# A hybrid backbone layer on one core: gate buffers, the block decays' row scale, the merges' buffers and the place of the 32-block solve

## The chip, the cores and the metric

The kernel runs on one core of a Trainium2 chip. The core has five engines with instruction streams of their own: TensorE (matmuls; PE in the profile, PEld for its weight loads), VectorE (DVE), ScalarE (ACT), GpSimd (POOL) and SyncE (SP, which here only issues DMAs). They meet through semaphores; each executes its own instructions strictly in the order in which they stand in the program. DMAs are issued from the queues of SP and of ScalarE. The metric is the device time of one execution in microseconds; a median over runs is given. Lower is better.

## The reference

One layer (DEPTH is 1) over 256 latent tokens and 256 context tokens of width 1024, all in float32: a half-step SwiGLU, a mixer, another half-step SwiGLU. The mixer runs two branches on the same projected input, a bidirectional gated delta rule (8 heads of 128) and a bidirectional Mamba-2 state-space scan (32 heads of 64, 2 groups), and merges them by sigmoid gates. The latent scan starts from the context's final state. The part that the change touches is the delta rule's triangular solve:

```python
    g = jnp.cumsum(blocks(g), axis=-1)
    decay = jnp.exp(jnp.where(causal, g[..., :, None] - g[..., None, :], -jnp.inf))
    kb = k * beta[..., None]
    a_mat = jnp.where(strict, jnp.einsum('bnhid,bnhjd->bnhij', kb, k) * decay, 0.0) + jnp.eye(CHUNK, dtype=f32)
    rhs = jnp.concatenate([v * beta[..., None], kb * jnp.exp(g)[..., None]], axis=-1)
    sol = lax.linalg.triangular_solve(a_mat, rhs, left_side=True, lower=True, unit_diagonal=True)
```

and, around it, in one call for each direction of each branch:

```python
    f = mixer_features(h, w_in[i], ...)
    o, _ = gdn_mixer(f, gdn_A_log[i], gdn_dt_bias[i], s_gdn)
    y, _ = ssd_mixer(f, mb_A_log[i], mb_dt_bias[i], s_mb)
    merged = jax.nn.sigmoid(ga) * (ya @ w_branch_gdn) + jax.nn.sigmoid(gb) * (yb @ w_branch_mb)
```

Queries, keys and values pass a depthwise convolution of five taps and SiLU first; queries and keys are normalised. The chunk is 64 tokens.

## The kernel before

The program goes through the adaptive-norm vectors and the first SwiGLU (until about 445 us), the mixer (until about 1050 us) and the second SwiGLU. A matmul in float32 precision is made of three passes with the operands split in a high and a low part (hH, hL, whi, wlo; lines L213 to L215): ScalarE copies a 512 KB weight tile to whi (L198), VectorE subtracts to get wlo (L202), both out of a ring of four raw tiles that SP loads (L192). Gates and zA are projected in one pass from the raw tile (`projf`, L611): 8 matmuls of 128x256 for each of 16 gate tiles.

*Keys and solve.* `keys` goes over the eight heads: a projection of 512 columns (256 context and 256 latent tokens), the convolution (`conv_silu`: L630 on VectorE is one tap, L635 the closing SiLU product, whose output is kcv for keys and cv for values), normalisation (L861, L872, L875) and the Gram matrices pg of each 128 tokens (L896). The Gram block goes by ScalarE's copy (L898) and a store (L899) to DRAM (Gsd), and comes back (L905) as N: 256 diagonal 32x32 blocks, 2 for each of 128 partitions. `block_decay` makes the matching decays D (two tiles of 32x32 entries for each partition): difference of the cumulated decays (L917, VectorE), a triangular select (L918, GpSimd), an exponential (ScalarE) and a product with -beta of the row, nb (L921, GpSimd). `elim` multiplies N by D (L963) and runs 30 steps of forward substitution, each one product into etmp (L967) and one addition to N (L970), all on VectorE. It stores the inverse blocks to DRAM (L973, Tsd).

*Merges.* `merge(s)`, for each of four pairs of 128-token tiles, one for each direction, reads those blocks back (L1102: TD and TT) and puts the 32-blocks together to 128x128 triangles. Lm holds Gram blocks, RA and RB decays (loaded from gsd, two subtractions on VectorE each, L1114, an exponential on ScalarE, L1116), which GpSimd multiplies into Lm (L1117). TensorE then goes through pTx (L1126), pTw (L1133), pTx (L1139), pTa, pTz and pTu. The zeros of TT and TD are written by VectorE (L1084 to L1088). `chain_step(s)` runs the scan over the pairs; steps 2 and 3 are the latent tokens and use `decay` (L932: a select by GpSimd into E, eight exponentials, a product with q k^T at L1200).

*Other work of that stretch.* `g_gen` is one gate tile: projection (L611), tanh on ScalarE (gth, L1071), store to gsc from ScalarE's queue (L1072). `dts` makes the step sizes of the state-space branch (softplus as a chain of 128x256 operations, L737 to L749, then pcd). `abdt` makes beta and the cumulated decays. v, q, xs, B, C, zB and zA are projected after the keys; then the state-space branch (`ssd_diag`, VectorE-heavy) and the two branches' output.

*What sets the order.* The functions emit their instructions in the order of the string PLAN (a token like `18/g5` sets the priority 18 and emits five gates; `k3` three keys; `13/m0` merge 0), and a scheduler then puts the instructions of each engine in an order by these priorities and by its own model of when each one is ready. So a change of PLAN, of a buffer or of an engine moves many instructions. A tile comes from a pool by a tag with a number of buffers, and a new tile of a tag waits until the last reader of the tile that held the buffer is done. The tags of this change: tZ, 2 buffers (gth, zth, dtx, dte); c4, 2 buffers (D, then the decays' gr and E); t4, 2 buffers (RA among others); tL, 2 buffers (sel, RB, dtz, dtg). PSUM tiles have tags too: mg has 2 banks (prow, pcd, the merges' products).

## Time and profile before

| | |
|---|---|
| time, median of 3 runs | 1342.9 us |
| the runs | 1342.9, 1339.09 and 5015.55 us |
| the profiled execution | 1346.67 us |
| its span (first to last instruction) | 1345.0 us |
| mean granted TensorE clock | 0.97 |
| busy: TensorE / VectorE / ScalarE / GpSimd | 96% / 71% / 37% / 12% |
| last key's Gram block (L896) | 516.75 us |
| solve: first product (L963) to last step (L970) | 528.35 to 591.01 us |
| first merge's first matmul (L1126) | 601.50 us |
| third run of the three | an outlier, which the median leaves aside |

The profile is of one execution on the chip. Rows of a timeline give start and duration in us, the engine, the line, the operation, the tile written and the tiles read, the shape, how many instructions stand in the row, and in brackets the engine's idle time ahead of it and what ended it. A float32 matmul is counted twice in the trace (a gate's 8 matmuls as 16). Durations of matmuls overlap, since they are pipelined: their pace is the difference of two starts. A row of the chain of waits gives start, duration, engine, tile and line. `SPq` is SP's queue.

### The profile page before, as it was taken

Reading aid. Unit: us, or ns where it says so; the run is one execution under the profiler, and the core shown is the slowest. Engines: PE = TensorE matmul, PEld = TensorE weight load, DVE = VectorE, ACT = ScalarE, POOL = GpSimd, SP = SyncE. Lnnn points to the kernel's source line nnn. Section 1 sums busy time; section 2 is a strip of 40 time slices with the busy share of each in tenths; the row PEclk is TensorE's granted clock in tenths of the full one; section 3 lists DMA queues with packets and bytes.
Section 4 is the critical chain, followed back from the end, with each engine's and each line's share of the span. In section 5 each row is a group of like instructions: output and inputs, shape, how many; then the busy total and the mean of one; then the engine's idle time right before and its main releaser. Section 6 shows DMA issues by size and latency. Waiting matters only on the chain.

```text
span 1345.0 us, 21303 instructions
## 1 busy us (share of the span) xinstructions
PE 1290.2 (96%) x8224; PEld 1108.4 (82%) x8224; DVE 955.1 (71%) x1666; ACT 501.3 (37%) x935; POOL 155.1 (12%) x123
## 2 busy tenths in 40 slices
...
GB/s 363 92 179 221 118 188 242 233 109 235 214 106 102 110 178 242 193 184 192 153 128 80 93 174 164 150 183 125 162 144 226 174 191 190 192 189 185 179 185 79
DMA packets 133018, 230.27 MB, mean 171 GB/s; under 512 B 46706, under 2 KB 78898, under 8 KB 132788
## 3 DMA queue, kind: packets, MB, share of 16 engines
...
## 4 chain that ended last, share of the span: by engine, by line
PE 64%; issue 15%; DVE 13%; DMA 5%; ACT 1%; POOL 1%; SPq 1%; DVEq 0%; POOLq 0%; ACTq 0%
PE acc L213 16%; PE acc L214 16%; PE acc L215 16%; PE acc L611 3%; PE pada L301 2%; DVE Es L1437 2%; DVE cv L630 2%; DVE Es L1426 1%; PE pn L1227 1%; PE pP L1218 1%; PE pS L1253 1%; DMA Es<-asd 1%; PE pTx L1139 1%; PE ptm L980 1%; DVE Es L1439 1%
## 5 line engine op out<-in xcount | busy, mean ns | idle before, releaser
L198 ACT CAST whi<-raw 128x1024 fp32r<-128x1024 f32 (+1 forms) x208 | 214.4, 1033 | 448.9 <-PE acc L214 397.7
L213 PE MATMUL acc<-hH,whi 128*128 128x512 f32 (+1 forms) x976 | 346.5, 357 | 3.6 <-ACT hH L432 1.8
L214 PE MATMUL acc<-hL,whi 128*128 128x512 f32 (+1 forms) x976 | 345.7, 354 | 0.0
L215 PE MATMUL acc<-hH,wlo 128*128 128x512 f32 (+1 forms) x976 | 344.8, 354 | 0.0
L202 DVE TENSOR_TENSOR wlo<-raw,whi 128x1024 fp32r<-128x1024 f32 (+1 forms) x208 | 251.3, 1210 | 96.1 <-ACT whi L198 94.3
L213 PEld LDWEIGHTS acc<-hH,whi 128*128 128x128 f32 x976 | 186.5, 191 | 27.8 <-ACT hH L432 2.2
L215 PEld LDWEIGHTS acc<-hH,wlo 128*128 128x128 f32 x976 | 186.6, 191 | 23.9
L214 PEld LDWEIGHTS acc<-hL,whi 128*128 128x128 f32 x976 | 186.6, 191 | 22.9
L270 DVE CUSTOM_DVE_ANT_0 junk<-wadat,cs 128x1024 f32<-128x1024 f32 x80 | 97.8, 1222 | 42.4 <-DMA wadat<-in_wadaT 41.7
L214 PE MATMUL acc<-aL,whi 128*128 128x256 f32 (+1 forms) x384 | 122.9, 323 | 0.0
L215 PE MATMUL acc<-aH,wlo 128*128 128x256 f32 (+1 forms) x384 | 122.3, 323 | 0.0
L213 PE MATMUL acc<-aH,whi 128*128 128x256 f32 (+1 forms) x384 | 122.2, 323 | 0.0
L630 DVE SCALAR_TENSOR_TENSOR cv<-cbuf,cc,cv 128x512 f32<-128x512 f32 (+1 forms) x144 | 107.3, 752 | 4.6 <-ACT cv L628 2.6
L611 PE MATMUL acc<-hF,raw 128*128 128x256 f32 x416 | 97.7, 391 | 8.4 <-ACT gth L1071 7.8
L611 PEld LDWEIGHTS acc<-hF,raw 128*128 128x128 f32 x416 | 80.8, 197 | 22.7 <-ACT gth L1071 9.1
L214 PEld LDWEIGHTS acc<-aL,whi 128*128 128x128 f32 x384 | 73.0, 190 | 5.6
L215 PEld LDWEIGHTS acc<-aH,wlo 128*128 128x128 f32 x384 | 72.7, 190 | 5.7
L213 PEld LDWEIGHTS acc<-aH,whi 128*128 128x128 f32 x384 | 72.6, 190 | 5.6
L567 DVE SCALAR_TENSOR_TENSOR xl<-acc,hg,xl 128x256 f32<-128x256 f32 x64 | 30.3, 482 | 47.0 <-PE acc L215 46.5
L1049 PE MATMUL acc<-raw,hF 128*128 128x512 f32 x128 | 59.4, 606 | 0.6 <-DVE zbt L1053 0.6
L372 POOL TENSOR_TENSOR sqa<-sqa,sqb 128x256 f32<-128x256 f32 x12 | 11.5, 962 | 410.6 <-ACT sqb L370 407.7
L1049 PEld LDWEIGHTS acc<-raw,hF 128*128 128x128 f32 x128 | 24.6, 194 | 30.5 <-issue 28.4
...
## 6 DMA issues: line engine op xcount, KB each, us to landing
...
```

What stands on the lines that cost most here:

```text
L198: nc.scalar.copy(hi, raw)
L202: engs[i % len(engs)].tensor_tensor(lo[:, c:c + w], raw[:, c:c + w], hi[:, c:c + w].bitcast(F32), op=ALU.subtract)
L213: mm(acc, wh, xh, start=start, stop=False)
L214: mm(acc, wh, xl, start=False, stop=False)
L215: mm(acc, wl, xh, start=False, stop=stop)
L270: self.nc.vector.tensor_tensor_reduce(out=self.junk, in0=w, in1=self.cs[s], scale=1.0, scalar=0.0, op0=ALU.mult, op1=ALU.add, accum_out=out)
L301: nc.tensor.matmul(pa[:, c], w[c][:, q * P:q * P + P], self.cTs[:, q], start=q == 0, stop=q == KD - 1)
L567: nc.vector.scalar_tensor_tensor(out=xs, in0=acc[:, NL * s - g0:NL * s - g0 + NL], scalar=hg[s][:, m:m + 1], in1=xs, op0=ALU.mult, op1=ALU ...
L611: self.nc.tensor.matmul(acc, w[:, k * P:k * P + P], self.hF[:, k], start=k == 0, stop=k == KD - 1)
L630: nc.vector.scalar_tensor_tensor(out=u3, in0=buf[:, 0:R, j:j + 64], scalar=cw[:, j:j + 1], in1=u3, op0=ALU.mult, op1=ALU.add)
L1049: nc.tensor.matmul(accs[t], self.hF[:, k, sl], w[:, wsl], start=k == 0, stop=k == 7)
L1437: V.scalar_tensor_tensor(out=B[:, j], in0=cb(1), scalar=col(self.dt, 1, j), in1=B[:, j], op0=ALU.mult, op1=ALU.add)
```

## The change

The rotation of some buffers and the place of some work change; what is computed stays the same, with the same matmuls.

- PLAN: the solve (`elim`) is emitted behind g5, dts, v2 and three further gates. The sixteen gates stay; the ten that followed v2 are split in three ahead of the solve and seven behind it.
- `g_gen`: gth gets a tag of its own with two buffers.
- `block_decay` loses the row product by nb. A new function `row_scale`, emitted just ahead of `elim`, transposes sel1 into a PSUM tile of its own, reduces it to nb and multiplies both D tiles on VectorE. sel1 becomes a constant tile, and the transpose and reduction of nb leave `abdt`.
- `keys`: the store of the Gram block is issued from ScalarE's queue and not from SP's.
- `merge`: six memsets for each merge go from VectorE to GpSimd, and RA takes a c4 buffer (where D was) and not a t4 buffer.

```diff
--- before.py
+++ after.py
@@ -28,7 +28,7 @@
 TAGS = dict(tA=4, tS=3, tL=2, tM=2, tZ=2)
 T4 = 2
 NCV = 2
-PLAN = """10/k3 block_decay k6 5/elim 18/g5 13/dts 20/v2 g10 v7 13/m0 14/m1 13/chain_start s0 s1 m2 m3 22/q9
+PLAN = """10/k3 block_decay k6 18/g5 13/dts 20/v2 g3 row_scale 5/elim 20/g7 v7 13/m0 14/m1 13/chain_start s0 s1 m2 m3 22/q9
     B_part 27/x17 25/lat_h 22/C_part 30/zB5 g17 zA9 chain_out 13/s2 s3 14/gdn_norm 15/ssd_pre h40 51/y0 gdn_out y1 70/mb_out"""
 NG = 5
 GQ = 0
@@ -80,7 +80,6 @@
 L2B = ("tr",)
 KL = ("dve",)
 MDE = 'vg'
-BDE = "vg"
 
 ADA_PE = [(k, c) for k in range(8) for c in range(2) if c or k < 4]
 
@@ -771,7 +770,8 @@
         V.tensor_scalar(out=alog, in0=alog, scalar1=-1.0, scalar2=None, op0=ALU.mult)
 
         gb = self.t2([P, 64], "gb", tag="tM")
-        sel = [self.t2([P, 16, 4, 2], f"sel{i}", tag="tL") for i in range(2)]
+        sel = [self.t2([P, 16, 4, 2], "sel0", tag="tL"), C([P, 16, 4, 2], "sel1")]
+        self.sel1 = sel[1]
         for q in sel:
             nc.gpsimd.memset(q, 0.0)
         halves = slice(0, 64), slice(64, P)
@@ -797,18 +797,15 @@
         V.tensor_copy(gc, pc[:, 0])
         for hb, hs in enumerate(halves):
             V.tensor_copy(sel[0][hs, :, :, hb], pc[hs, 0].rearrange("p t u -> p u t"))
-        pr = self.smp([P, 3, P], "prow", "mg")
+        pr = self.smp([P, 2, P], "prow", "mg")
         nc.tensor.transpose(pr[0:64, 0], gb, self.ident)
-        for i, q in enumerate(sel):
-            q = q.rearrange("p u t b -> p (u t b)")
-            nc.tensor.transpose(pr[:, 1 + i], q, self.ident)
+        nc.tensor.transpose(pr[:, 1], sel[0].rearrange("p u t b -> p (u t b)"), self.ident)
         rows = self.t2([64, P], "rows", tag="tM")
         nc.scalar.copy(rows, pr[0:64, 0])
         nc.scalar.dma_start(self.gsd, rows)
 
         self.gn, self.nb = C([P, 64], "gn"), C([P, 64], "nb")
-        for i, q in ((1, self.gn), (2, self.nb)):
-            V.tensor_reduce(out=q, in_=pr[:, i].rearrange("p (b c) -> p c b", b=2), op=ALU.add, axis=AX.X)
+        V.tensor_reduce(out=self.gn, in_=pr[:, 1].rearrange("p (b c) -> p c b", b=2), op=ALU.add, axis=AX.X)
         V.tensor_scalar(out=self.gn[64:P], in0=self.gn[64:P], scalar1=-1.0, scalar2=None, op0=ALU.mult)
         self.gcA = C([P, 4, 16], "gcA")
         V.tensor_copy(self.gcA, gc)
@@ -896,7 +893,7 @@
                 nc.tensor.matmul(pg[:, t], kT[:, ts], kT[:, ts], start=True, stop=True)
             G = kb([P, 4, P])
             nc.scalar.copy(G, pg)
-            nc.sync.dma_start(self.Gsd[h, :, 0:P].rearrange("t r c -> r t c"), G)
+            nc.scalar.dma_start(self.Gsd[h, :, 0:P].rearrange("t r c -> r t c"), G)
             if h in NB:
                 h0 = max([0] + [q + 1 for q in NB if q < h])
                 src = self.Gsd[h0:h + 1].rearrange("h t r c -> (h t r c)").rearrange("(p s x) -> p s x", s=2, x=32 * (P + 1))
@@ -908,8 +905,8 @@
     def block_decay(self):
 
         nc, G = self.nc, self.nc.gpsimd
-        gn, nb = self.gn, self.nb
-        BS, BM = (nc.vector if c == "v" else G for c in BDE)
+        gn = self.gn
+        BS = nc.vector
         self.D = []
         for sb in range(2):
             D = self.c4([P, 32, 32], "D")
@@ -918,8 +915,17 @@
             G.affine_select(out=D, in_=D, pattern=[[1, 32], [-1, 32]], base=0, channel_multiplier=0,
                             compare_op=ALU.is_gt, fill=-1e30)
             nc.scalar.activation(D, D, AF.Exp)
-            BM.tensor_tensor(D, D, self.bc(nb[:, 32 * sb:32 * sb + 32], 32, 32), op=ALU.mult)
             self.D.append(D)
+
+    def row_scale(self):
+
+        nc, V = self.nc, self.nc.vector
+        pr = self.smp([P, P], "prow", "mg")
+        nc.tensor.transpose(pr, self.sel1.rearrange("p u t b -> p (u t b)"), self.ident)
+        nb = self.nb
+        V.tensor_reduce(out=nb, in_=pr.rearrange("p (b c) -> p c b", b=2), op=ALU.add, axis=AX.X)
+        for sb, D in enumerate(self.D):
+            V.tensor_tensor(D, D, self.bc(nb[:, 32 * sb:32 * sb + 32], 32, 32), op=ALU.mult)
 
     def decay(self, t, d):
 
@@ -1067,7 +1073,7 @@
     def g_gen(self):
         for m in range(16):
             acc = self.projf("wg", m)
-            th = self.t2([P, NL], "gth", tag="tZ")
+            th = self.tp.tile([P, NL], F32, tag="gth", bufs=2, name="gth")
             self.nc.scalar.activation(th, acc, AF.Tanh, scale=0.5)
             self.nc.scalar.dma_start(self.gsc[m], th)
             yield
@@ -1081,14 +1087,15 @@
         idl, idh = self.ident[lo, lo], self.ident[hi, hi]
         TT = [self.tt([P, 8, P], f"TT{d}") for d in range(2)]
         TD = self.t2([P, 8, 64], "TD", tag="tM")
-        V.memset(TT[0][hi, :, lo], 0.0)
-        V.memset(TT[1][lo, :, hi], 0.0)
+        Z0 = nc.gpsimd.memset
+        Z0(TT[0][hi, :, lo], 0.0)
+        Z0(TT[1][lo, :, hi], 0.0)
         for r in (0, 64):
-            V.memset(TT[1][r:r + 32, :, r + 32:r + 64], 0.0)
-            V.memset(TD[r:r + 32, :, 32:64], 0.0)
+            Z0(TT[1][r:r + 32, :, r + 32:r + 64], 0.0)
+            Z0(TD[r:r + 32, :, 32:64], 0.0)
         Lm = self.tp.tile([P, 16, 96], F32, tag="lm", bufs=1, name="Lm")
         L21, L10 = Lm[:, :, 0:64], Lm[:, :, 64:96]
-        RA, RB = self.t4([P, 16, 64], "RA"), self.t2([P, 16, 32], "RB", tag="tL")
+        RA, RB = self.c4([P, 16, 64], "RA"), self.t2([P, 16, 32], "RB", tag="tL")
         q4 = [slice(32 * i, 32 * i + 32) for i in range(4)]
         c2 = [slice(0, 32), slice(32, 64)]
         part = lambda d, q: TD[q4[q], :, c2[q % 2]] if d == 0 else TT[1][q4[q], :, q4[q]]
```

Where these move instructions, on TensorE behind the last key's Gram block (L611 is a gate matmul, L980 a transpose of a value tile, L843, L844 and L850 belong to `dts`). Before, from 12 projection matmuls behind that block to the last gate of this stretch:

```order
L611 MATMUL acc<-hF,raw 128x256 x8
L980 MATMUL ptm<-ident,cv_3398 128x128 x4
L611 MATMUL acc<-hF,raw 128x256 x20
L843 MATMUL pcd<-dtg,UT 128x4x32
L843 MATMUL pcd<-dtg,LT 128x4x32
L844 MATMUL pcd<-dtg,ones 128x256
L611 MATMUL acc<-hF,raw 128x256 x11
L850 MATMUL prow<-ident,gc 128x128
L611 MATMUL acc<-hF,raw 128x256 x41
```

Now, from the last key's Gram block on (L893 is L896 of before, L610 is L611, L986 is L980):

```order
L893 MATMUL pg<-kT 128x128 x4
L610 MATMUL acc<-hF,raw 128x256 x5
L986 MATMUL ptm<-ident,cv_3396 128x128 x4
L610 MATMUL acc<-hF,raw 128x256 x17
L986 MATMUL ptm<-ident,cv_3397 128x128 x4
L610 MATMUL acc<-hF,raw 128x256 x58
```

The same 80 gate matmuls stand there, now without `dts`' products, which have moved ahead, among the keys. Ahead of the Gram block TensorE has 12 more projection matmuls of the values than before.

On TensorE at the first merge's first matmul (pTx; 128x512 is a projection of values, 128x256 one of queries). Before:

```order
L213 MATMUL acc<-hH_3151,whi 128x512
L214 MATMUL acc<-hL_3153,whi 128x512
L215 MATMUL acc<-hH_3151,wlo 128x512
L1126 MATMUL pTx<-ident,TD 32x32 x8
L1126 MATMUL pTx<-ident,TT_4671 32x32 x8
L1126 MATMUL pTx<-ident,TD 32x32 x8
L1126 MATMUL pTx<-ident,TT_4671 32x32 x8
```

and now (L1133 is L1126 of before):

```order
L212 MATMUL acc<-hH_3151,whi 128x256
L213 MATMUL acc<-hL_3153,whi 128x256
L214 MATMUL acc<-hH_3151,wlo 128x256
L1133 MATMUL pTx<-ident,TD 32x32 x8
L986 MATMUL ptm<-ident,cv_3397 128x128 x4
L212 MATMUL acc<-hH_3067,whi 128x256
L213 MATMUL acc<-hL_3069,whi 128x256
```

Before, no query projection stands ahead of the first merge; now 72 matmuls of it do, and 16 more transposes of values.

On VectorE at the beginning of the solve (L963 is the product with D, L967 and L970 a step; L746 to L749 and L840 belong to `dts`; L630 and L635 to a value's convolution). Before:

```order
L963 TENSOR_TENSOR N<-N,D 128x1024 x2
L630 SCALAR_TENSOR_TENSOR cv_3399<-cbuf_3293,cc,cv_3399 128x512
L746 SCALAR_TENSOR_TENSOR dt<-dt,dtz 128x256
L967 TENSOR_TENSOR etmp<-N 128x60
L630 SCALAR_TENSOR_TENSOR cv_3399<-cbuf_3293,cc,cv_3399 128x512
L747 SCALAR_TENSOR_TENSOR dt<-dt,dte 128x256
L970 TENSOR_TENSOR N<-N,etmp 128x2x30
L749 SCALAR_TENSOR_TENSOR dt<-dt,dtx 128x256
L967 TENSOR_TENSOR etmp<-N 128x116
L635 SCALAR_TENSOR_TENSOR cv_3399<-cv_3399 128x512
L840 TENSOR_TENSOR dtg<-dt,alogs 128x256
L970 TENSOR_TENSOR N<-N,etmp 128x2x29x2
```

and now (L969, L973 and L976 are L963, L967 and L970 of before; L1121 is L1114):

```order
L969 TENSOR_TENSOR N<-N,D 128x1024 x2
L973 TENSOR_TENSOR etmp<-N 128x60
L976 TENSOR_TENSOR N<-N,etmp 128x2x30
L973 TENSOR_TENSOR etmp<-N 128x116
L976 TENSOR_TENSOR N<-N,etmp 128x2x29x2
L973 TENSOR_TENSOR etmp<-N 128x168
L976 TENSOR_TENSOR N<-N,etmp 128x2x28x3
L973 TENSOR_TENSOR etmp<-N 128x216
L976 TENSOR_TENSOR N<-N,etmp 128x2x27x4
L973 TENSOR_TENSOR etmp<-N 128x260
L976 TENSOR_TENSOR N<-N,etmp 128x2x26x5
L973 TENSOR_TENSOR etmp<-N 128x300
```

The solve's first steps stand next to each other now. The operations of `dts` stand among the keys, the first subtraction of RA behind the eleventh half-step, and the subtractions of the first RB pairs ahead of the solve. Behind this piece, among the later steps, stand 20 convolution taps (12 before) and nine weight splits (six before).

## The prediction

> **What bounds the kernel now.** I read the page first, then TensorE's and VectorE's busy time in stretches, then TensorE's timeline where it stands idle, then the chain and the queues of that place. The page:
>
> ```profile
> PE 1290.2 (96%) x8224; PEld 1108.4 (82%) x8224; DVE 955.1 (71%) x1666; ACT 501.3 (37%) x935; POOL 155.1 (12%) x123
> ```
>
> TensorE is busy for 1290.2 of 1345.0 us. The change takes no matmul away, so all that it can win are TensorE's 55 us of idle time and the time at a lower clock. Stretches (PE, PEld, DVE, ACT, POOL busy, then the granted clock, the DMA share and GB/s) show where that is in the part that the change reorders, from about 445 to 1050 us:
>
> ```profile
> 475.00:500.00 25.00, 20.96 (x106) 18.58 (x105) 20.97 (x27) 14.20 (x40) 10.44 (x6) 0.87 0.90 186
> 525.00:550.00 25.00, 17.15 (x70) 14.36 (x69) 19.49 (x35) 6.78 (x16) 3.44 (x2) 0.80 0.71 160
> 950.00:975.00 25.00, 19.65 (x58) 9.96 (x57) 23.30 (x51) 6.69 (x14) 10.36 (x9) 0.86 0.35 120
> ```
>
> Two of the holes are ones that the change aims at. TensorE's timeline:
>
> ```profile
> 494.20 1.12 PE L861 MATMUL l2t<-ident,kcv 128*128 128x128 f32 x4 [4.04 <-DVE kcv L635]
> 497.67 6.59 PE L611 MATMUL acc<-hF,raw 128*128 128x256 f32 x24
> 516.75 1.05 PE L896 MATMUL pg<-kT 128*128 128x128 f32 x8
> 535.73 8.11 PE L611 MATMUL acc<-hF,raw 128*128 128x256 f32 x24 [7.85 <-ACT gth L1071]
> 549.41 18.25 PE L611 MATMUL acc<-hF,raw 128*128 128x256 f32 x82
> 601.50 0.69 PE L1126 MATMUL pTx<-ident,TD 32*32 32x32 f32 x16
> ```
>
> L611 is a gate: 8 matmuls, which the trace counts as 16. At full clock one record takes 18.25 / 82 = 0.223 us, a matmul 0.445, a gate 3.56. Behind both waits the clock is down: the 24 records at 535.73 take 8.11 us and not 5.35 (2.8 lost), those at 497.67 6.59 (1.2 lost, and some 1.8 more in the three rows ahead, since the L896 pass there takes 1.92 us against 1.05 at 516.75, and L861 and L875 twice their usual time). So the second hole costs 7.85 + 2.8 = 10.6 us, the first 4.04 + 3.0 = 7.0.
>
> But work of another kind is nearly as late as TensorE there. The chain of waits from the last key's Gram block (L896) to the 32-block solve on VectorE, and the solve's end with the queue that carries it to the first merge:
>
> ```profile
> 516.91 0.91 PE pg L896 x8
> 517.84 0.60 ACT kb L898
> 518.45 4.03 DMA Gsd<-kb
> 523.86 4.49 DMA Lm<-Gsd
> 528.35 2.36 DVE N L963 x2
> ...
> 590.79 0.22 DVE L970 TENSOR_TENSOR N<-N,etmp 128x60 f32<-128x60 f32 x1
> ...
> 591.03 0.33 SPq L973 DMA_DIRECT2D Tsd<-N  x1
> 596.61 1.80 SPq L1102 DMA_DIRECT2D TD<-Tsd  x4
> 598.46 2.45 SPq L1102 DMA_DIRECT2D TT<-Tsd  x5
> ```
>
> The solve runs from 528.35 to 591.0. Its blocks are stored and loaded back by SP; the TT loads are issued until 600.9, and the merge's first matmul (L1126) starts at 601.50. TensorE came there without idle time, so it was not early: the solve was ready with it, to within a microsecond. Whoever takes 10.6 us from TensorE ahead of that place must also bring the solve forward, or TensorE waits at L1126 instead.
>
> **The change part by part.** *Own buffers for the gates' tanh.* Before, gth takes turns with dtx and dte in tZ, so a gate's tanh waits until VectorE is done with the dt chain, which itself is spread around the solve's start:
>
> ```profile
> 510.88 0.29 DVE L836 COPY dtx<-dt 128x256 f32<-128x256 f32 x1 [4.79 <-DMA gsc<-gth]
> 531.29 2.56 DVE L746 SCALAR_TENSOR_TENSOR dt<-dt,dtz 128x256 f32<-128x256 f32 x1
> 535.11 1.28 DVE L749 SCALAR_TENSOR_TENSOR dt<-dt,dtx 128x256 f32<-128x256 f32 x1
> DMA to landing us min/median/max: 2.2/3.5/6.7
> ```
>
> The wait at 535.73 ends with dtx's last reader, L749. With two own buffers a tanh waits only for the store of the gate two before it; that store lands in 2.2 to 6.7 us (last row), and two gates take 7.1. I take the wait as gone: -10.6 (bounds: 0, were a store to take longer, and -10.6).
>
> *Keys' stretch (450 to 520).* The dt chain (ten 128x256 operations, a reciprocal) moves ahead of the solve, among the keys' convolutions. By its rows that is some 8 us of VectorE, and the row multiply D*nb adds 2 x 1.2 (L963's two of that size take 2.36). Four subtractions of RA (0.69 each, 2.8), and the memsets (seven groups of 0.48 to 0.64, 3.8) leave. And GpSimd's own D*nb no longer slows VectorE:
>
> ```profile
> 483.83 2.29 DVE L630 SCALAR_TENSOR_TENSOR kcv<-cbuf,cc,kcv 128x512 f32<-128x512 f32 x1
> 486.15 2.29 DVE L1114 TENSOR_TENSOR RA<-gcA,RA 64x512 f32<-64x512 f32 x1
> 489.08 0.74 DVE L630 SCALAR_TENSOR_TENSOR kcv<-cbuf,cc,kcv 128x512 f32<-128x512 f32 x1
> ...
> 483.19 4.70 POOL L921 TENSOR_TENSOR D<-D,nb 128x1024 f32<-128x1024 f32 x2
> ```
>
> Two operations lose 1.55 and 1.6 us beside it, a third about 1.0: 4.1. Sum: 10.4 - 2.8 - 3.8 - 4.1 = about 0. So the keys come neither sooner nor later by work alone, and the stall of 7.0 may go or double. I take -3 (bounds -7 and +7). The memsets cost GpSimd nothing that anyone waits for: it is busy 12%. The Gsd stores that go from SP to ScalarE's queue take one issue each; the last of them was not late before (kb ends 518.44, store at 518.45), so 0.
>
> *The solve.* What TensorE's matmuls cost, by the chain (512 columns, then transposes in fours) and the timeline (256 columns; two such start 0.12 us apart):
>
> ```profile
> 592.90 0.23 PE acc L215
> 593.13 0.44 PE ptm L980 x4
> ...
> 604.85 0.28 PE L214 MATMUL acc<-hL,whi 128*128 128x256 f32 x1
> 604.97 0.28 PE L215 MATMUL acc<-hH,wlo 128*128 128x256 f32 x1
> ```
>
> In the new order TensorE has 12 more projection matmuls of 512 columns and four small ones ahead of the last L896 (12 x 0.23 + some 0.7 = 3.5 us), so the solve starts 3.5 later. Between L963 and the solve's last step VectorE had, by counts and durations of this profile, 52.7 us of work; now 61.1: the dt chain and four RB subtractions are out, two convolution units, three weight splits (L202) and more RA subtractions in. Before, 52.7 of work took 62.4 us, with four waits that add up to 4.1 us (one is shown) and some 5 lost beside GpSimd's L1117 (L746 and L749 above take 2.1 and 0.9 us more than the 0.4 that their neighbours of that size take, L970 here 0.95 more than the 0.66 of the step ahead, an RB subtraction 1.1):
>
> ```profile
> 554.68 0.43 DVE L1114 TENSOR_TENSOR RB<-gcA,RB 128x256 f32<-128x256 f32 x1 [1.13 <-DMA RB<-gsd]
> 557.30 1.61 DVE L970 TENSOR_TENSOR N<-N,etmp 128x480 f32<-128x480 f32 x1
> ...
> 531.24 2.34 POOL L1117 TENSOR_TENSOR Lm<-Lm,RA 64x1024 f32<-64x1024 f32 x1 [30.15 <-DMA Lm<-Gsd]
> 556.80 3.23 POOL L1117 TENSOR_TENSOR Lm<-Lm,RB 32x512 f32<-32x512 f32 x2 [20.69 <-ACT RB L1116]
> ```
>
> With as many waits and as much loss the new one takes 62.4 + 8.4 = 70.8; with half of both 66.4. I take 69: its end is 3.5 + 6.6 = 10 us later. TensorE also has more to do ahead of the first merge: 72 matmuls of 128x256 (0.12 each, 8.6 us), 16 small ones (1.8) and three of 0.23: 11.1. So it arrives at 601.5 - 10.6 + 11.1 = 602, the solve's blocks at 611.5. TensorE stands for 9.5 us, and by the 2.8 that followed the 7.85 loses about 3 more: +12.5 (bounds: 0 if the solve keeps its old length, +17 with 70.8 and waits besides). The 11.1 us of work done early aren't lost: they are missing later.
>
> On the loss beside GpSimd, the Trainium skill (SBUF — State Buffer, "Who interferes with whom") says that the shared pair of ports is an exclusive lock, so that the later of two instructions fully blocks. In the rows here 5.57 us of L1117 cost some 5, nearly a full block. In the new solve GpSimd has two of the RA kind and one pair of RB, 7.9 us: by the rule all of it is lost, and the solve takes 61.1 + 7.9 = 69.0 with no wait for a load, 73.1 with as many as before, which would put the sum at 0. The page adds that the two-input operations collide only with a GpSimd operation that reads SBUF, which the moved memsets don't.
>
> *RA in the D tiles' slots (c4).* RA's load can now be issued only behind L963, and the decays of chain steps 2 and 3 wait for the merges. In VectorE's order RA's first subtraction stands 3.5 us of work behind L963, its load takes 0.6 + 3.1 to 7.5: that is among the waits above. Further on, the first decay's product L1200 stands on VectorE some 12 us of work behind merge 2's last TT, while its E comes by Lm's load (4.5), both parts of L1117 (2.3 + 3.2), a select and eight exponentials of 0.387 (3.1; then the landing of RA's loads):
>
> ```profile
> L936 ACT ACTIVATE E<-E,ngc x32: 384/387/403, 537.4 to 833.4; 128x128 f32<-128x128 f32 x32
> DMA to landing us min/median/max: 3.1/4.5/7.5
> ```
>
> That is 13.1 us and the select, so VectorE waits 2 to 5 us with the chain's L1229 behind it; TensorE has projections there. I take +2 (bounds 0 and +9).
>
> *Tail.* 22 of the 64 zA matmuls move ahead of the last diagonal block, into a stretch in which VectorE sets the pace (TensorE 19.65 of 25 busy at 950). Before, all stood behind it:
>
> ```profile
> 999.99 7.13 PE L611 MATMUL acc<-hF,raw 128*128 128x256 f32 x32
> ```
>
> 22 x 0.445 = 9.8 is the most; the zA results are then stored and loaded once more, which doesn't shrink. I take half, -5 (bounds -9.8 and 0).
>
> Sum: -10.6 - 3 + 12.5 + 2 - 5 = -4.1. The profiled execution took 1346.67 us (span 1345.0 and 1.7 around it), 3.8 above the median of the runs, 1342.9. So 1342.6 for a profiled one, 1338.8 for the median: I say **1339**.
>
> **The rivals.** *A, the solve is not late.* VectorE had idle time around 505 and 514 and loses less to GpSimd, so that the solve may end by 592; then TensorE finds its blocks ready and the whole gain stays. For it: the dt chain's waits are gone. Against it: 8.4 us more work in front of the last step, in order. Time: 1342.9 - 10.6 - 3 + 2 - 5 = 1326, and a short stall with its clock makes it some us more. What a short stall costs is itself open:
>
> ```profile
> 650.65 1.65 PE L1253 MATMUL pS<-ch,ch 128*128 128x128 f32 x6 [2.06 <-DVE ch L1229]
> 650.00:700.00 50.00, 47.91 (x568) 43.42 (x569) 34.97 (x83) 17.00 (x35) 8.94 (x7) 0.93 0.43 130
> ```
>
> The Trainium skill (TensorE: Matmul & The Clock Gate, "What's actually happening") lets the clock fall after an idle window of about 3.4 us. The rows differ: 2.06 us idle are followed by a clock of 0.93 over 50 us, which is 7 us at half. By the rule a stall of 2 us costs 2; by the rows some 5.
>
> *B, slower: the shared c4 slots.* Place: VectorE's queue in the solve and at L1200. Each RA load must wait for a D tile or for an earlier merge's L1117, and stands on SP between gate weights that wait for TensorE. If two rounds of RA land after 7.5 instead of 4.5 us behind SP's other loads, the solve ends 5 to 7 us later still; L1200 at its upper bound adds 7. Together +12 to +14 on the sum: 1351 to 1353. It decides from some 8 us of such waits beyond those I took: below that the kernel stays under 1347. For it: SP loads waited for in the solve's rows above. Against it: the new order puts the subtractions later too.
>
> *C, the gates still wait.* Should the tanh stores land late, beside the Gsd stores in ScalarE's queue, the 10.6 stay, but then TensorE meets the solve at L1126 on time, as before: 1338 to 1343, no other time than the forecast's. That the gates' wait is no price of its own follows from the solve.
>
> **How the numbers follow.** The forecast (the wait moves to the first merge, C with it) gets 0.52 and 1330 to 1347; A 0.26 with 1316 to 1330; B 0.16 with 1347 to 1360; the rest, 0.06, is further out on either side. The range from 1320 to 1356 leaves out the outer part of A (0.07), of B (0.05) and the rest. A measurement of this kernel can tell about 2% from no change, 1316.0 and 1369.8: beyond the first lies only the case that A meets the upper bounds of both the keys' stretch and the tail (-7, -9.8: 1317), 0.06; beyond the second a B with new waits in later merges, 0.04.
>
> **What would show it.** Right: no wait of L611 for gth; the last L896 some 3 us later, or as much earlier as the keys' stall shrinks; the solve's last step some 69 us behind L963; an idle time of TensorE of 6 to 12 us ahead of L1126 with a clock below 1 in that stretch. Wrong: L1126 without idle time and the last step within 64 us of L963 (A), or RA's subtractions with waits above 3 us each and a wait at L1200 (B). The step that I trust least is the length of the solve.

## The result and the profile after

The changed kernel takes 1336.45 us (median of 20 runs) beside 1343.12 us for the kernel before (20 runs on the same chip). The ratio is 0.9947, with a 95% interval of 0.9931 to 0.9964: 7.1 us less, between 4.8 and 9.3. That lies within 2%, but the interval excludes no change. One run of each kernel (5015.55 and 2520.34 us) lies far out; the medians hardly feel it, and the ratio is made without it.

The profiled execution has a span of 1334.0 us (1335.7 with the 1.7 us around it), 0.7 below its median; the one of before was 3.6 above its own. So the two profiles differ by 11.0 us, and some 4 of these are scatter. The mean granted clock rose from 0.970 to 0.982. The page's line of busy times, after the change:

```profile
PE 1279.7 (96%) x8224; PEld 1100.2 (82%) x8224; DVE 940.9 (71%) x1644; ACT 502.3 (38%) x935; POOL 157.4 (12%) x145
```

TensorE executes the same 8224 matmuls in 10.5 us less busy time. None of them was taken out or made smaller, so what is gone is time at a lower clock. To see where, the stretches of both kernels (start and end; length; PE, PEld, DVE, ACT, POOL busy with the number of instructions; granted clock; DMA share; GB/s). The first goes from the keys to 20 us behind the first merge's first matmul, the second over the rest of the merges, the third over the state-space branch, the fourth over the mixer's end. Before:

```profile
445.00:620.00 175.00, 162.33 (x994) 139.75 (x994) 141.93 (x250) 83.09 (x220) 23.94 (x16) 0.95 0.71 189
620.00:780.00 160.00, 153.36 (x1659) 136.55 (x1655) 117.73 (x226) 63.46 (x133) 34.43 (x26) 0.95 0.41 122
860.00:1000.00 140.00, 129.00 (x426) 70.36 (x424) 120.06 (x222) 39.48 (x91) 58.74 (x40) 0.94 0.46 155
1000.00:1060.00 60.00, 53.49 (x292) 48.01 (x292) 23.17 (x40) 17.56 (x32) 5.79 (x5) 0.91 0.58 191
```

After, with the first two ends moved by 14 and 4 us, since the merges come later:

```profile
445.00:634.00 189.00, 173.97 (x1080) 150.50 (x1078) 148.63 (x264) 88.22 (x227) 26.91 (x26) 0.97 0.69 194
634.00:784.00 150.00, 148.48 (x1636) 130.37 (x1635) 105.54 (x210) 67.41 (x141) 35.18 (x38) 0.99 0.42 124
860.00:1000.00 140.00, 126.39 (x434) 70.32 (x433) 118.54 (x215) 36.29 (x84) 53.60 (x37) 0.96 0.48 161
1000.00:1060.00 60.00, 53.84 (x335) 49.58 (x335) 28.80 (x48) 21.40 (x35) 6.28 (x5) 0.94 0.58 197
```

TensorE's idle time is a stretch's length less its busy time. Up to the first merge, where the change works, it has not shrunk: 12.7 us before, 15.0 after. In the merges it fell from 6.6 to 1.5, and the clock there rose from 0.95 to 0.99. Below, *loss* is TensorE's idle time plus half of the busy time that the clock records put at half clock, summed from the traces over stretches that end at marks of each kernel (last Gram block; first pTx and 20 us; last pTu and 3 us; last matmul of the diagonal blocks; 1060 us):

| loss, us | before | after |
|---|---|---|
| 445 to the last Gram block | 7.0 | 7.3 |
| on to the first merge | 11.3 | 12.6 |
| the rest of the merges | 14.7 | 3.1 |
| state-space branch (860 on) | 18.8 | 17.6 |
| the mixer's end | 10.6 | 9.6 |
| sum | 62.5 | 50.2 |

The sum falls by 12.3, beside 11.0 between the two profiles. Nearly all of it is in the merges. Split the other way, idle time hardly differs over the five stretches (36.8 and 36.3 us), since the 5.1 us that the merges lost are made up elsewhere; time lost at half clock fell from 25.7 to 13.9, of it 8.1 to 1.6 in the merges. So between these two profiles the gain lies in fewer spells of low clock and not in fewer waits in all.

What stood there is told by the table of TensorE's waits (who waits and for what: total us, times, the longest). Before, 620 to 780 us:

```profile
PE pS L1253 <- DVE ch L1229: 2.1, 1, 2.1
PE pn L1227 <- ACT ch L1233: 1.6, 1, 1.6
PE pTa L1148 <- ACT TD L1141: 1.2, 1, 1.2
PE acc L213 <- ACT cv L628: 0.8, 1, 0.8
PE pTa L1147 <- ACT TD L1141: 0.5, 1, 0.5
...
```

After, 634 to 784 us:

```profile
PE pP L1225 <- DVE E L1207: 0.6, 1, 0.6
PE pS L1260 <- DVE ch L1236: 0.3, 1, 0.3
PE acc L212 <- ACT cv L627: 0.3, 1, 0.3
...
```

The waits for a merge's own small steps (TD) are gone and that for the chain's ch has all but gone. The two waits for ch weighed most. The clock records have half clock behind both (650.4 to 657.2 and 732.3 to 742.5 us) and none behind the 1.18 us for TD, so that with it they make up some 11.7 of the 14.7 us lost. VectorE's timeline of the kernel before shows what delayed the first:

```profile
649.18 0.69 DVE L1114 TENSOR_TENSOR RA<-RA,gcA 64x512 f32<-64x512 f32 x1 [3.31 <-DMA RA<-gsd]
649.91 0.69 DVE L1229 TENSOR_TENSOR ch<-pn,wk 128x512 f32<-128x512 f32 x1
```

The chain's step (L1229) stood behind a subtraction of RA, which waited 3.31 us for RA's load, and was done 4.8 us behind the last pn. TensorE had 2.8 us of other small matmuls (pTw, pS) in between. In the changed kernel the same kind of matmuls stands there, for 2.7 us; a subtraction of RA waits 1.25 us, ch is done 3.0 us behind pn, and TensorE stands for 0.30. So this wait went because VectorE came sooner, not because TensorE had more to do meanwhile. The second (731.82) came behind three convolution taps that took 5.46 us on VectorE, where a tap beside no product of GpSimd took 0.74 (the row at 489.08 in the prediction).

At the wait for TD, TensorE's cover, that is, the work it has between two steps of a chain, did change. TensorE's timeline between two steps of merge 1, pTx and pTa: before, 22 query matmuls of 256 columns stand there:

```profile
660.60 0.39 PE L213 MATMUL acc<-hH,whi 128*128 128x256 f32 x1
...
663.43 0.33 PE L1147 MATMUL pTa<-ident,TD 64*64 64x64 f32 x2
665.59 0.27 PE L1148 MATMUL pTa<-ident,TD 64*64 64x64 f32 x1 [1.18 <-ACT TD L1141]
```

They last 2.8 us, TD comes later, and TensorE stands for 1.18. After, 20 value matmuls of 512 columns stand at the same place, 4.7 us, and pTa finds TD ready:

```profile
668.34 0.48 PE L212 MATMUL acc<-hH,whi 128*128 128x512 f32 x1
...
673.08 0.33 PE L1154 MATMUL pTa<-ident,TD 64*64 64x64 f32 x2
```

The 72 query matmuls that the new order puts ahead of the first merge leave the long projections of values for the merges behind it. But TD also came sooner: its second copy on ScalarE was done 1.6 us behind the last pTx, and 4.9 us before, where a weight cast (L198, 664.11 to 665.15) and two exponentials of RB stood ahead of it. The short cover would have been enough for 1.6 us, so this pair doesn't show what the long cover is worth.

The gates' wait, which the change aims at, has another cause now but is not gone. TensorE's timeline after the change:

```profile
507.30 0.79 PE L212 MATMUL acc<-hH,whi 128*128 128x512 f32 x1 [4.00 <-ACT gth L1077]
...
540.75 12.31 PE L610 MATMUL acc<-hF,raw 128*128 128x256 f32 x48 [3.80 <-ACT gth L1077]
...
554.78 3.72 PE L610 MATMUL acc<-hF,raw 128*128 128x256 f32 x16 [1.72 <-ACT gth L1077]
...
559.49 7.17 PE L610 MATMUL acc<-hF,raw 128*128 128x256 f32 x32 [0.99 <-ACT gth L1077]
```

ScalarE's timeline and the chain of waits tell why the second tanh was late (L989 is the store of a value tile, on ScalarE's queue):

```profile
539.83 0.38 ACTq L989 DMA_DIRECT2D vsc<-vt  x1
540.31 0.38 ACT L1077 ACTIVATE gth<-acc 128x256 f32<-128x256 f32 x1 [7.04 <-DMA Lm<-Gsd]
```

```profile
524.95 5.30 DMA Gsd<-kb
...
530.27 4.43 DMA N<-Gsd
...
534.71 5.04 DMA Lm<-Gsd
...
539.83 0.38 ACTq L989
```

The tanh stood behind the store of L989, and that store's issue waited until Lm's load, which SP had issued, had landed (539.76). By the trace's records both DMAs count on semaphore 105, and the issue waits for it; the load's last count came at 539.76. The wait at 507.30 is of the same kind: ScalarE's Gram store was issued at 503.64, right behind the landing of the Gram store ahead of it (503.56), and the tanh followed it.

The solve, by VectorE's timeline:

```profile
536.28 2.36 DVE L969 TENSOR_TENSOR N<-N,D 128x1024 f32<-128x1024 f32 x2 [7.31 <-DMA N<-Gsd]
...
548.10 2.66 DVE L976 TENSOR_TENSOR N<-N,etmp 128x336 f32<-128x336 f32 x1
...
603.21 0.23 DVE L976 TENSOR_TENSOR N<-N,etmp 128x60 f32<-128x60 f32 x1
```

From its first product to its last step it takes 67.2 us (62.7 before) and ends 12.4 later. At the first merge TensorE comes later too, and hardly stands for it (its timeline again):

```profile
604.50 0.66 PE L986 MATMUL ptm<-ident,cv 128*128 128x128 f32 x4 [1.34 <-ACT vt L988]
605.84 0.89 PE L986 MATMUL ptm<-ident,cv 128*128 128x128 f32 x4 [0.69 <-ACT vt L988]
...
614.43 0.69 PE L1133 MATMUL pTx<-ident,TD 32*32 32x32 f32 x16
...
618.91 0.59 PE L1133 MATMUL pTx<-ident,TT 32*32 32x32 f32 x13 [0.58 <-DMA TT<-Tsd]
```

### The profile page after: what moved, and what is told of

The parts are those of the page before. It is cut to its first block, busy times and chain, and to the rows that moved or that the text cites. A ratio compares the mean times of both kernels' runs of the same rounds, so it can differ in the third digit from the quotient of the medians.

```text
span 1334.0 us, 21300 instructions
## 1 busy us (share of the span) xinstructions
PE 1279.7 (96%) x8224; PEld 1100.2 (82%) x8224; DVE 940.9 (71%) x1644; ACT 502.3 (38%) x935; POOL 157.4 (12%) x145
## 4 chain that ended last, share of the span: by engine, by line
PE 66%; issue 16%; DMA 7%; DVE 7%; ACT 3%; POOL 1%; SPq 0%; ACTq 0%; POOLq 0%; DVEq 0%
PE acc L212 16%; PE acc L213 16%; PE acc L214 16%; PE acc L610 3%; PE acc L1055 2%; PE pada L300 2%; DVE Es L1433 2%; DVE cv L629 1%; DMA Es<-asd 1%; PE pn L1234 1%; PE pS L1260 1%; PE pP L1225 1%; PE pyd L1449 1%; DMA raw<-in_wv 1%; DMA zA<-zAsc 1%
## 5 line engine op out<-in xcount | busy, mean ns | idle before, releaser
L629 DVE SCALAR_TENSOR_TENSOR cv<-cbuf,cc,cv 128x512 f32<-128x512 f32 (+1 forms) x144 | 100.6, 711 | 5.7 <-ACT cv L627 3.9
L610 PE MATMUL acc<-hF,raw 128*128 128x256 f32 x416 | 95.6, 385 | 7.1 <-ACT gth L1077 6.5
L610 PEld LDWEIGHTS acc<-hF,raw 128*128 128x128 f32 x416 | 78.8, 193 | 19.5 <-ACT gth L1077 7.7
L1055 PEld LDWEIGHTS acc<-raw,hF 128*128 128x128 f32 x128 | 24.5, 194 | 29.6 <-issue 28.4
```

The lines of the kernel that those rows point to most:

```text
L610: self.nc.tensor.matmul(acc, w[:, k * P:k * P + P], self.hF[:, k], start=k == 0, stop=k == KD - 1)
L629: nc.vector.scalar_tensor_tensor(out=u3, in0=buf[:, 0:R, j:j + 64], scalar=cw[:, j:j + 1], in1=u3, op0=ALU.mult, op1=ALU.add)
L1055: nc.tensor.matmul(accs[t], self.hF[:, k, sl], w[:, wsl], start=k == 0, stop=k == 7)
```

## The experiments

The question was which part of the change brings the gain, and why it appears in the merges, where nothing was expected. Four theories in words: (1) up to the first merge the solve's chain sets the time, so taking a wait from TensorE there gives nothing; (2) RA's c4 slot alone brings the merges' gain; (3) the order string brings it, since it puts queries ahead of the first merge, and gth's own buffers are what that order needs; (4) no part does, only several together. All kernels compute what the reference does. Each ratio is to the kernel before, timed on the same chip; the losses are made as in the table above. So "loss to first merge" goes from 445 us to 20 us behind the first pTx and holds what is lost in the merge's first steps too. "Queries ahead" are the 256-column query matmuls that TensorE executes before the first pTx, "Gram to step" the time from the last Gram block to the solve's first step.

| kernel | us | ratio (95%) | loss to first merge | merges | 860 on to 1060 | Gram to step | queries ahead |
|---|---|---|---|---|---|---|---|
| before | 1343.1 | 1 | 18.4 | 14.7 | 29.4 | 16.3 | 0 |
| after | 1336.5 | 0.9947 (0.9931 to 0.9964) | 20.0 | 3.1 | 27.2 | 16.7 | 72 |
| before, RA in c4 | 1349.1 | 1.0047 (1.0026 to 1.0067) | 20.3 | 17.2 | 28.8 | 17.9 | 0 |
| before, new order | 1354.8 | 1.0098 (1.0059 to 1.0137) | 34.0 | 3.4 | 33.8 | 27.4 | 48 |
| before, gth buffers | 1347.0 | 1.0029 (1.0006 to 1.0053) | 18.4 | 14.3 | 29.9 | 15.5 | 0 |
| before, order and gth | 1350.9 | 1.0045 (1.0017 to 1.0074) | 26.6 | 8.4 | 34.4 | 18.7 | 48 |
| before, queries early | 1342.0 | 0.9975 (0.9952 to 0.9998) | 24.0 | 6.7 | 23.7 | 16.5 | 72 |
| after, store on SP | 1337.9 | 0.9956 (0.9935 to 0.9977) | 22.6 | 3.2 | 28.7 | 21.0 | 54 |
| after, D*nb on GpSimd | 1339.7 | 0.9949 (0.9930 to 0.9969) | 20.5 | 8.2 | 28.4 | 17.0 | 72 |
| after, RA in t4 | 1342.4 | 0.9994 (0.9970 to 1.0017) | 23.1 | 9.5 | 31.5 | 19.7 | 48 |
| after, memsets on VectorE | 1344.3 | 1.0003 (0.9983 to 1.0023) | 22.2 | 8.3 | 29.6 | 17.1 | 49 |
| after, old order | 1348.4 | 1.0037 (1.0018 to 1.0056) | 23.8 | 9.4 | 30.8 | 20.9 | 0 |
| after, gth in tZ | 1354.9 | 1.0084 (1.0058 to 1.0110) | 31.9 | 5.1 | 29.7 | 30.5 | 46 |
| after, queries earlier still | 1358.9 | 1.0092 (1.0061 to 1.0123) | 28.3 | 8.1 | 34.2 | 17.2 | 72 |

One profile scatters. "After" and "after, D*nb on GpSimd" have the same order on TensorE and the same time, yet 3.1 and 8.2 in the merges. Differences of 5 us in one cell therefore carry nothing by themselves; 14 against 3, or 32 against 20, do. The four kernels with the lowest ratios (the first of them "after") lost 13.9 to 19.2 us at half clock, the other ten 20.2 to 29.5; in idle time the four (35.9 to 38.0) hardly stand apart from the best of the others (36.8, 37.5, 37.7). The medians of before differ from job to job (1342.4 to 1345.8), so kernels are compared by their ratios. Two of the expectations below give 3.6 us for the merges of the changed kernel, where the table has 3.1; nothing hangs on the difference.

**Single parts on the kernel before.** RA in c4:

```diff
-        RA, RB = self.t4([P, 16, 64], "RA"), self.t2([P, 16, 32], "RB", tag="tL")
+        RA, RB = self.c4([P, 16, 64], "RA"), self.t2([P, 16, 32], "RB", tag="tL")
```

> The kernel before with one part of the change: RA takes a c4 buffer. The two traces show that TensorE's idle time and slow clock between the first merge and 780 us fell from 14.7 to some 4 us, and that nothing was won ahead of the first merge. Theory M (the merges' stalls came from RA's late load and from decays standing between the merges on GpSimd, both a matter of RA's slot): the stalls of 602 to 780 us fall to 6 or less, 1333 to 1338 us. Theory O (they went because projections were done early, as filler ahead of the first merge): the stalls stay, 1341 to 1346. Theory G (the prediction: what counts is the gates' wait): 1341 to 1350, since RA's load now waits for the solve's start.

Measured: 1349.1 us, ratio 1.0047. The merges' loss is 17.2, not less than before's 14.7. Theory 2 falls: no subtraction of RA waits for its load by more than 0.33 us in these merges, but other waits stand there (2.07 us for TD, 2.01 us for ScalarE, 1.58 us for the decay's E).

The order string alone (`row_scale` doesn't exist here; nb is made in `abdt` as before):

```diff
-PLAN = """10/k3 block_decay k6 5/elim 18/g5 13/dts 20/v2 g10 v7 13/m0 ...
+PLAN = """10/k3 block_decay k6 18/g5 13/dts 20/v2 g3 5/elim 20/g7 v7 13/m0 ...
```

> The kernel before with one part of the change: the solve emitted behind three gates (the order string), D*nb staying in the block decays on GpSimd. Theory O: the 48 query matmuls that now stand ahead of the first merge and the other filler in the merges remove the stalls there, 1334 to 1339 us. Theory M: the stalls of the merges stay, since RA keeps its t4 buffer, and the solve has 13 more rows of other work inside it: 1341 to 1348. Theory G: the gates' wait at 528 us stays, since tZ is still shared: 1341 to 1346.

Measured: 1354.8 us, 1.0098. The merges do lose only 3.4 now, but 15.6 more are lost ahead of them, since the solve's first step comes 27.4 us behind the last Gram block. VectorE's timeline of this kernel shows what is late:

```profile
508.86 0.29 DVE L836 COPY dtx<-dt 128x256 f32<-128x256 f32 x1 [7.39 <-DMA gsc<-gth]
...
540.62 0.42 DVE L846 COPY gc<-pcd 128x256 f32<-128x256 f32 x1 [2.53 <-PE pcd L844]
```

dtx stood 7.39 us for a gate's store, because it takes its buffer from gth; and `dts`' last part (pcd) runs into the solve.

gth's buffers alone:

```diff
-            th = self.t2([P, NL], "gth", tag="tZ")
+            th = self.tp.tile([P, NL], F32, tag="gth", bufs=2, name="gth")
```

> The kernel before with one part of the change: own buffers for the gates' tanh. Theory G: the wait of 7.85 us and the slow clock behind it go, and the solve is no later than before (fewer other rows stand inside it, 87 against 97): 1331 to 1337 us. Theory M: ScalarE stood behind the value's SiLU (L633, which waits for VectorE) as long as behind tZ, so a wait of several us remains, and the merges' stalls stay: 1339 to 1344.

Measured: 1347.0 us, 1.0029. The loss to the first merge is 18.4, the same as before, and the first pTx comes at 602.5 (601.5 before). But own buffers didn't free the gates. TensorE's timeline of this kernel, and ScalarE's ahead of the second wait:

```profile
500.68 6.61 PE L611 MATMUL acc<-hF,raw 128*128 128x256 f32 x16 [4.65 <-ACT gth L1071]
548.71 16.85 PE L611 MATMUL acc<-hF,raw 128*128 128x256 f32 x64 [4.70 <-ACT gth L1071]
```

```profile
545.00 2.45 ACT L936 ACTIVATE E<-E,ngc 128x128 f32<-128x128 f32 x8 [7.04 <-POOL E L932]
```

The two waits add up to 9.35 us, more than the 7.85 before. The second tanh stood on ScalarE behind the decay's exponentials, which waited 7.04 us for GpSimd; the first stood behind an exponential of RA, which waited 2.71 us for VectorE. So theory 1 is not tested here, since no wait was taken from TensorE; the "wait of several us" of the expectation's theory M came. That the time is some us longer isn't accounted for by the losses (62.6 in all, 62.5 before).

**Undoing one part of the change.** The Gram store back on SP's queue:

```diff
-            nc.scalar.dma_start(self.Gsd[h, :, 0:P].rearrange("t r c -> r t c"), G)
+            nc.sync.dma_start(self.Gsd[h, :, 0:P].rearrange("t r c -> r t c"), G)
```

> The changed kernel with one part undone: the Gram block's store is issued by SP again. In the changed kernel ScalarE's queue stood at 503.6 and 508.9 us until an earlier store had landed, with a gate's tanh behind it, and TensorE lost 4.0 us at 503 and 1.7 at half clock. Theory H (ScalarE's queue is held by DMAs that wait for landings): that idle time goes, 1330 to 1335 us. Rival (the wait only moves to SP's queue, in front of the gate weights): TensorE waits for raw weights instead, 1335 to 1341.

Measured: 0.9956, not to be told from 0.9947. The stall among the keys all but vanishes (loss 1.3 and not 7.3), which confirms that the store's issue on ScalarE's queue makes it. The last Gram block comes 8.9 us sooner (512.28 and not 521.21), but the loads behind it are slower, and the solve's first step stands 21.0 us behind it. The DMAs of 505 to 545 us by kind (how many, KB each, median us from issue to landing), in this kernel:

```profile
N<-Gsd SPq DMA_DIRECT2D x4, 128.0 KB, 8.6
```

and in the changed one:

```profile
N<-Gsd SPq DMA_DIRECT2D x5, 128.0 KB, 5.2
```

At the first merge TensorE waits for the solve's blocks, 0.53 us for TD and then for TT (timeline):

```profile
614.69 0.59 PE L1133 MATMUL pTx<-ident,TT 32*32 32x32 f32 x13 [1.61 <-DMA TT<-Tsd]
```

The 6 us that TensorE lost less among the keys came back, and more (8.7), in the stretch behind them, but only in part as theory 1 has it: the waits for the solve's blocks grew by 1.6 us. The rest is a wait of 2.27 us for a gate's raw weights (530.66), which is the rival of the expectation, 1.1 us more at the transposes of values, and 4.7 us more at half clock; the gates' waits stay (0.73 and 4.91). The time, 1337.9, lies in the rival's range and not in theory H's.

The old order in the changed kernel, with `row_scale` ahead of `elim`:

```diff
-PLAN = """10/k3 block_decay k6 18/g5 13/dts 20/v2 g3 row_scale 5/elim 20/g7 v7 13/m0 ...
+PLAN = """10/k3 block_decay k6 row_scale 5/elim 18/g5 13/dts 20/v2 g10 v7 13/m0 ...
```

> The changed kernel with one part undone: the order string of before (the solve ahead of the gates; the row scale stands directly in front of it). No query matmul stands ahead of the first merge now, 72 did. Theory O (projections done early leave the wider ones as cover in the merges): the loss of TensorE in the merges, 3.6 us in the changed kernel and 14.7 before, goes back to 9 or more, and the time to 1341 to 1347. Theory S (only the solve's end counts; here 12 taps and 8 splits stand inside it and not 20 and 9): the first merge comes earlier, 1331 to 1336.

Measured: 1.0037 (1348.4 us). No query matmul stands ahead of the first merge, and the merges lose 9.4, with 4.5 more until 860 us, where the changed kernel loses nothing. The first merge does come sooner (600.5), as theory S has it, but the time goes up as theory O has it, and a little beyond.

RA back in t4 (the first diff, reversed):

> The changed kernel with one part undone: RA takes a t4 buffer again, so that the first decay's select stands on GpSimd ahead of the merges, and RA's subtractions ahead of the solve. 48 query matmuls stand ahead of the first merge. Theory M (RA's slot is part of the gain in the merges): their loss goes up from 3.6 to 8 or more, 1340 to 1345. Theory O: it stays at 5 or less and the solve is shorter without RA's four subtractions: 1333 to 1338.

Measured: 0.9994 (1342.4 us), so the gain goes, and the merges' 9.5 is what theory M expected. The losses rise by 3.1, 6.4 and 4.3: no one place. This run shows best what theory 1 says: TensorE comes to the first merge 10.3 us sooner than in the changed kernel (604.1), the blocks only 6.9 sooner (TT is there at 611.97 and not 618.91), and TensorE loses 10.0 us in the 20 behind the first pTx, 3.64 of it waiting for TT and 5.8 at half clock. The solve ended 9.6 us sooner (593.9); between its store and TT's loads SP's queue issued weights and the chain's loads. So the blocks' way through that queue is part of the bound, and not the solve alone.

gth back in tZ (the third diff, reversed):

> The changed kernel with one part undone: the gates' tanh shares tZ with the dt chain. Where the order string alone was changed, 27 us lay between the last Gram block and the first step of the solve, and not 16, and the time was 1354.8. Theory B (with the solve behind the gates, the dt chain waits on VectorE for a gate's store, in front of the solve; own buffers are what the new order needs): the same here, 24 us or more, 1343 to 1352. Rival (the delay has another cause): 16 to 18 us, 1334 to 1340.

Measured: 1.0084, the worst of the undone parts. VectorE's timeline:

```profile
506.17 0.29 DVE L833 COPY dtx<-dt 128x256 f32<-128x256 f32 x1 [5.17 <-DMA gsc<-gth]
...
535.07 0.29 DVE L926 TENSOR_REDUCE nb<-prow 128x64 f32<-128x128 f32 x1 [6.85 <-PE prow L924]
```

With the shared tag the dt chain waits for two gates' stores (5.17 us, and 3.50 at 509.96), the reduction to nb waits for its transpose, and the solve's first step comes 30.5 us behind the last Gram block and not 16.7. The loss to the first merge is 31.9. So the own buffers do not free the gates; they free VectorE's dt chain, which the new order puts ahead of the solve.

The memsets back on VectorE, and D*nb on GpSimd at the same place:

```diff
-        Z0 = nc.gpsimd.memset
+        Z0 = V.memset
```

> The changed kernel with one part undone: the merges' zeros are written by VectorE. 49 query matmuls stand ahead of the first merge. If VectorE's time among the keys matters, its 3.8 us of memsets there make the last Gram block 2 to 4 us later, and the time 1338 to 1342. If what bounds the stretch is ScalarE's queue and the loads, nothing changes: 1334 to 1339.

```diff
-            V.tensor_tensor(D, D, self.bc(nb[:, 32 * sb:32 * sb + 32], 32, 32), op=ALU.mult)
+            self.nc.gpsimd.tensor_tensor(D, D, self.bc(nb[:, 32 * sb:32 * sb + 32], 32, 32), op=ALU.mult)
```

> The changed kernel with one part undone: D*nb runs on GpSimd again, at the same place, everything else in the same order. If GpSimd's 4.7 us slow VectorE's operations beside them as before (4 us lost), and the solve's start hangs on VectorE: first step 3 to 5 us later, 1338 to 1342. If the solve's start hangs on the Gram blocks' way through memory (VectorE waited 7.3 us for it in the changed kernel): the same start, 1335 to 1338.

Measured: 1.0003 (1344.3 us) and 0.9949 (1339.7 us). The place of D*nb carries nothing: the first step comes as in the changed kernel, 17.0 us behind the Gram block. For the memsets both forecasts missed: the last Gram block came 5.5 us sooner and not later, and the time is above both ranges. Taking the memsets back costs the whole gain by the ratio, as RA's slot does, but it also makes the scheduler order TensorE otherwise (49 queries ahead and not 72), so their own price isn't separated from that.

**Two parts together, and the cover alone.** The order and gth's buffers on the kernel before (the second and third diffs):

> The kernel before with two parts of the change together: the order string and the gates' own buffers. The order string alone gave 1354.8 us, the buffers alone 1347.0. Theory B (in the new order the dt chain's tiles and the gates' must not share a slot): 16 to 18 us from the last Gram block to the solve's first step (27 with the order alone), TensorE's loss up to the first merge 18 to 22 us (34 with the order alone), and in the merges 5 or less as with the order alone: 1334 to 1339. Rival (RA's slot and the memsets are needed as well): 8 or more lost in the merges, 1340 to 1346.

Measured: 1350.9 us, 1.0045, where 1334 to 1339 was expected. The buffers bring the solve forward (18.7 us behind the Gram block, 27.4 without them) and the ratio from 1.0098 to 1.0045, but the loss to the first merge is still 26.6. Of it 8.4 us stand behind the first pTx, which comes at 610.1; ahead of it TensorE loses 18.1, as before. So theory 3 holds for what the buffers do and fails as the whole account: something else of the change is needed too, which is theory 4. The undone parts point at RA's slot and the memsets; no run adds these two to the pair.

Queries ahead of the last value heads in the kernel before, and nothing else:

```diff
-PLAN = """10/k3 block_decay k6 5/elim 18/g5 13/dts 20/v2 g10 v7 13/m0 14/m1 13/chain_start s0 s1 m2 m3 22/q9
+PLAN = """10/k3 block_decay k6 5/elim 18/g5 13/dts 20/v2 g10 v3 q3 v4 13/m0 14/m1 13/chain_start s0 s1 m2 m3 22/q6
```

> The kernel before with nothing of the change: only three query heads are emitted ahead of the last four value heads, so that 72 query matmuls (128x256) stand ahead of the first merge, as in the changed kernel, and value matmuls (128x512) take their place as cover in the merges. All up to the last Gram block, RA's slot and GpSimd's order stay as before. Theory O: TensorE's loss in the merges falls from 14.7 to 6 or less, with 18 to 19 up to the first merge: 1332 to 1337 us. Rival (the merges' stalls come from RA, the memsets or GpSimd): 10 or more, 1340 to 1346.

Measured: 1342.0 us, 0.9975 (1332 to 1337 was expected). The merges' loss falls from 14.7 to 6.7, and TensorE's waits from 624 to 794 us are down to these:

```profile
PE pTw L1133 <- POOL Lm L1117: 0.9, 1, 0.9
PE ptm L980 <- ACT vt L982: 0.7, 1, 0.7
PE ptm L980 <- ACT qT L876: 0.5, 1, 0.5
```

The waits for ch and TD are gone, without any other part of the change. But the loss ahead of the first merge rises by 5.6, so that little is left. So an order with queries early takes loss out of the merges, and its net size was overestimated. That the wide cover does it isn't shown: where the kernel before waited for TD, 16 query matmuls of 256 columns stand here, 4.0 us, and TD's second copy was done 1.7 us behind pTx. Over all fourteen kernels, the four without queries ahead lose 9.4 to 17.2 us in the merges, the ten with 46 or more 3.1 to 9.5.

The same move added to the changed kernel:

```diff
-... 5/elim 20/g7 v7 13/m0 14/m1 13/chain_start s0 s1 m2 m3 22/q9
+... 5/elim 20/g7 v3 q3 v4 13/m0 14/m1 13/chain_start s0 s1 m2 m3 22/q6
```

> The changed kernel with three query heads emitted ahead of the last four value heads: 96 value and 72 query matmuls ahead of the first merge (144 and 72 in the changed kernel), 11 us less. Theory O with the solve as the bound up to the first merge: nothing is left to win in the merges (3.1 us), and TensorE, with 11 us less to do, stands longer at the first merge: 1338 to 1346. If TensorE and not the solve is late there: 1331 to 1336.

Measured: 1358.9 us, 1.0092 (1338 to 1346 was expected). TensorE now meets ScalarE, which hasn't yet read the projection's PSUM (2.94 us at 587.85, and then, by the timeline):

```profile
595.93 0.80 PE L212 MATMUL acc<-hH,whi 128*128 128x512 f32 x1 [3.63 <-ACT cv L627]
```

It makes the stretch ahead of the merge 8.3 us worse, without a gain behind it. None of the twelve kernels is faster than the changed one; two (the store on SP, D*nb on GpSimd) can't be told from it, and the interval of a third (queries early on the kernel before) overlaps with its own.

**What stays open.** Each of the three parts that were put on the kernel before alone (RA's slot, the order, gth's buffers) made it slower, and so did the pair; the memsets, the store and the row scale were not put there alone. Why the memsets and RA's slot matter together with the others isn't settled: each edit lets the scheduler reorder many instructions, and no run holds that order fixed while it moves only the memsets or only RA. For the same reason the 3 to 8 us by which the losses from 860 us on differ between kernels are not explained.

## Why the prediction was right or wrong

The time was forecast as 1339.0 and measured as 1336.45, inside the range and near the likeliest value. The account behind it had the balance of its two largest terms right and each of the two wrong, and lacked the term that brings the gain.

*The gates' wait, -10.6, and the first merge, +12.5.* Together +1.9, and the loss from the last Gram block to the first merge did change by +1.3. That fits the step that whoever takes time from TensorE ahead of that place must also bring the solve forward, and RA back in t4 shows it for the blocks, if not for the solve's end: TensorE comes 10.3 us sooner, TT 6.9, and 10.0 are lost there. In the changed kernel itself the step wasn't put to the test, since each half was wrong: the gates still wait (3.80 + 1.72 + 0.99 us), so TensorE comes to the merge at 614.4 and not at 602, and stands 0.58 us and not 9.5. That is rival C in what happened; its time, 1338 to 1343, was counted with the forecast's, and it put the wait down to stores that land late. The failed step is "I take the wait as gone". The prediction had only looked at the buffers' readers. But a tanh also waits for whatever stands ahead of it in ScalarE's queue, among it issues of DMAs that wait for other DMAs. The kernel before with own buffers alone shows this: two waits for a tanh, 4.65 and 4.70 us, behind exponentials that waited for VectorE and GpSimd.

The reading of before was incomplete in the same way. ScalarE's timeline of the kernel before, at the end of the wait of 7.85 us:

```profile
534.77 0.63 ACT L633 ACTIVATE cv<-cv 128x512 f32<-128x512 f32 x1 [12.08 <-DVE cv L630]
535.31 0.37 ACT L1071 ACTIVATE gth<-acc 128x256 f32<-128x256 f32 x1
```

The tanh that ended the wait stood behind a convolution's activation that had waited 12.08 us for VectorE. The prediction put the wait down to the buffer's reader L749, which ran from 535.11 to 536.39, so it was not yet done when this tanh began. Two causes lay within about a microsecond there, and to take away the buffer's leaves the queue's. The next tanh, at 536.47, came right behind L749's end.

*The solve's length.* 69 forecast, 67.2 measured. Its start was sized wrong: 536.28, not 531.9. The Gram block came at 521.21, 4.5 later than before (3.5 forecast), and the way to the product took 15.1 us and not 11.6: the copy stood behind ScalarE's convolution work and the store landed in 5.30 and not 4.03. The two errors cancel in part: its end is 603.4, beside 601 by the sum. Of the waits that the sum took over from before (4.1 us), 0.86 us is left, and GpSimd's products there take 5.0 us and not the 7.9 that the sum had. For the loss beside GpSimd the row is the step at 548.10: 2.66 us beside a merge product of 2.36, where the product of the same length (L973) ahead of it took 0.51. That is 2.15 lost of 2.36. It agrees with the exclusive lock that the Trainium skill (SBUF — State Buffer, "Who interferes with whom") states, though the sum by that rule with as many waits as before, 73.1, was too long.

*The keys, -3.* The loss went from 7.0 to 7.3. The work on VectorE did balance, as the sum said, but a new wait of 4.00 us stands in the old one's place, made by the Gram stores. The step "the Gsd stores that go from SP to ScalarE's queue take one issue each ... so 0" failed: an issue costs its queue also the wait for the DMA ahead of it. With the store on SP that loss was 1.3.

*RA's slot, +2.* In the merges TensorE waited 0.6 us for the decay's E and lost 1.6 at half clock behind it, and RA's first subtraction waited for nothing. Rival B didn't come; its sign is seen only where c4 stands alone (1.0047). 

*The tail, -5.* The losses fell by 1.2 from 860 us to the last diagonal block and by 1.0 behind it: -2.2. The right sign, half the size.

*What was left out, -11.6.* The prediction counted the 11.1 us of queries ahead of the first merge as work that is only missing later. It didn't ask what the new order does to the chain of small steps in the merges, though it showed the wait of 2.06 us there. "Queries early" shows that such an order alone takes 8.0 us of the merges' loss away; since one profile scatters by some 5, its share in the 11.6 isn't known closer. Whether the longer cover or the earlier steps on VectorE and ScalarE do it stays open; at that wait of 2.06 us it was VectorE's step, and the cover was nearly the same.

*Why the sum still came out.* Measured by loss: +0.3 keys, +1.3 to the first merge, -11.6 merges, -2.2 tail, in sum -12.2; by the ratio of the timed runs -7.1. Forecast: -4.1. Of the -10.6 that was hoped for at the gates some 2 us of waiting went (behind the last Gram block 8.5 us before, 6.5 after), a new wait for a tanh came among the keys, and a gain of the same size came where none was counted. The 1339 was near the result by luck.

*The clock.* Stretches of the changed kernel that follow idle times of 3.80 us and of 1.34 + 0.69 us (columns as above, clock third from the end):

```profile
541.00:545.00 4.00, 4.00 (x12) 3.21 (x12) 3.83 (x6) 0.38 (x1) 2.66 (x2) 0.57 1.08 242
606.00:610.00 4.00, 3.80 (x20) 3.40 (x20) 3.59 (x7) 1.73 (x4) 0.00 (x0) 0.57 1.02 410
```

Both halve the clock. So waits of 1 to 2 us did cost more than themselves, as the row of before had it that the prediction showed (2.06 us idle). An idle window of about 3.4 us, by which the Trainium skill (TensorE: Matmul & The Clock Gate, "What's actually happening") lets the clock fall, wasn't needed at 606. The length of a wait alone doesn't decide: in the changed kernel half clock from 749.46 to 752.87 follows one wait of 0.60 us, and in the kernel before none follows the 1.18 us at 665.59. Matmuls of 32x32 (pTx, from 746.93 on) stand ahead of the former; whether their size plays a part is not shown. Such spells are why the short waits in the merges were worth 11.6 us: the idle time there fell by 5.1 and the time lost at half clock by 6.5.
